# Pinning a program's first loads to program order and moving modulation rows and a broadcast behind them

## The chip, the cores and the metric

The kernel runs on one core of one Trainium2 chip. The metric is the device time of one execution in microseconds (us). Before the change it is 2306.07 us, the median of 3 runs (2305.83 to 2308.95).

## What is computed

A backbone of four layers over 256 latent tokens and 256 context tokens of width 1024, in float32. Each layer has a token mixer (chunked gated MLP, neighbourhood attention, mLSTM, chunked gated MLP) and a squared-ReLU MLP. Both are wrapped in RMSNorm and adaLN: a vector (c for the latent tokens, c_ctx for the context) passes a silu and a 1024 x 6144 matrix `ada_w`, and gives shift, scale and gate per layer:

```python
mod = [m[:, None, :] for m in jnp.split(c_act @ ada_w[i] + ada_b[i], 6, axis=-1)]
h = rmsnorm(x, norm_g[i, 0]) * (1.0 + mod[1]) + mod[0]
y = chunk_gmlp(h, ...)                       # layer 0
x = x + mod[2] * rmsnorm(y, norm_g[i, 1])
h = rmsnorm(x, norm_g[i, 2]) * (1.0 + mod[4]) + mod[3]
x = x + mod[5] * rmsnorm(sqrelu_mlp(h, ffn_w1[i], ffn_w2[i]), norm_g[i, 3])
```

So the first projection of layer 0 needs mod[0] and mod[1] of that layer for both vectors; mod[2] to mod[5] are needed later.

## The kernel before

The 512 tokens are four tiles of 128: two of context (`CTXT`), two latent (`LAT`). Weights arrive as tiles of 128 x 1024 float32 (512 KB): `raw`, four buffers. ScalarE copies such a tile to `whi` (rounded to float32r, L1288), VectorE computes the rest `wlo` (L1289), four buffers each; TensorE multiplies hi by hi, hi by lo and lo by hi (L391 to L393, one "step" of four token tiles is 24 matmuls of row blocks for two slices of 128). The activations are split in the same way into `hhi` and `hlo` (`split_h`, L336 and L337).

The modulation of a layer comes in two ways. By TensorE (`pe_items`, L200): `ada_w` itself is loaded into the same `raw` buffers and multiplied with silu(c) as a stationary operand of 32 columns; mod[0] and mod[1] of layer 0 come this way, in two groups `("s", 0)` and `("s", 1)` of eight raws, each group giving both mods for half of the channels. After a group, `ada_sum` (L222) copies the sum out of PSUM on ScalarE, `ada_fin` (L236 to L248) transposes it on TensorE and finishes on VectorE. By VectorE (`row_items`, L170): a transposed tile of `ada_w` (`row`, three buffers) is multiplied with `crow`, which is silu(c) broadcast to all partitions, and summed along the row; two such operations, one for each vector, make a block of 128 channels. mod[2], mod[3], mod[4] of layer 0 come this way, 24 tiles, spread over the first half of layer 0's mixer. `load_crow` (L146) loads c and c_ctx to 128 partitions, 512 KB each, and takes the silu.

The plan (`plan`) is a list of steps in program order. In layer 0: the first group's raws, sums of squares and transposes of the context tiles (`rows(CTXT)`, L1125 to L1143), loads and the same for the latent tiles, `apply` (modulate and split) for one half of the channels, the first two steps of the projection `gv` for the context tiles and then for the latent ones, with the second group's raws between, `apply` for the other half, and then the rest. The projection's results go through four PSUM buffers (`py`) that VectorE evacuates (L515). `emit` walks through the list and issues loads some steps ahead (`AHEAD`): list 0 holds the weights and the raws, list 1 the modulation rows.

Program order is not the order on an engine: a scheduler of the framework sorts the instructions of each queue by what it thinks is ready, loads and modulation rows too. Each queue then runs strictly in its order. Loads of the `raw` and `row` tiles go through SP's queue, some small ones and the two broadcasts of c through ScalarE's, bias rows through GpSimd's. A load on SP's or ScalarE's queue also takes one of eight semaphores in turn, and waits until the load that had it before has landed.

Of the kernel before, what the change touches and what calls it, by code (L numbers as in the profile page):

```python
# [8 lines left out]
F = mybir.dt.float32  # L9
# [14 lines left out]
CTXT = (0, 1)  # L24
LAT = (2, 3)
NB_HI = 4
NB_RAW = 4
NB_ROW = 3
LOOK = 3

AHEAD = (3, 2)
# [14 lines left out]

ON_PE = [(1, 5), (2, 5), (3, 2), (3, 5)]
FILLS = {(0, 0): (2, 2), (0, 1): (1, 1), (1, 0): (2, 1), (1, 1): (3, 2), (2, 0): (5, 0), (2, 1): (4, 0), (3, 0): (7, 0)}
XS1, XS2 = 2, 3
WAIT = 3  # L50
S2B, NUMB = 6, 2

# [10 lines left out]
class Net:  # L63
# [27 lines left out]

    def py(self):
        return self.pp.tile([128, 512], F, tag="py", bufs=4, name=self.name("py"))

    def w4(self):
        return self.sp.tile([128, 1024], F, tag="w4", bufs=2, name=self.name("w4"))
# [49 lines left out]
    def load_crow(self):  # L146

        for s in range(2):
            self.nc.scalar.dma_start(self.crow[:, s], self.bc(self.t["crow"][s]))
        self.nc.scalar.activation(self.crow, self.crow, AF.Silu)  # L150

    def new_mods(self, l):
# [950 lines left out]
    def plan(self):  # L1103
        nc, t = self.nc, self.t
        L = self.layers
        steps = []

        def load_xs(g):
            for i in g:
                if g == CTXT:  # L1110
                    x = self.w4()
                    self.xs[i] = [x[:, :512], x[:, 512:]]
                else:
                    self.xs[i] = [self.w2(), self.w2()]
                for h in range(2):
                    nc.sync.dma_start(self.xs[i][h], t["xin"][i][:, h * 512:(h + 1) * 512])

        def start():
            self.xs = {}
            load_xs(CTXT)  # L1120
            nc.sync.dma_start(self.ident, t["ident"])
            self.new_h()
            self.xT = self.ybuf()[:, :4096].rearrange("p (k n) -> p k n", k=8)

# [30 lines left out]

        first = self.pe_items(L[0], ("s", 0), True) + self.pe_items(L[0], ("s", 1), True)
        f0, f1 = first[:6], first[6:]
        steps += f0[:XS1] + [Step(lambda: load_xs(LAT))] + f0[XS1:XS2] + [Step(lambda: rows(CTXT))] + f0[XS2:]
        later = [x for u in ON_PE if u[0] in L for x in self.pe_items(*u)]

        def take(c):
# [5 lines left out]
        for n, l in enumerate(L):  # L1167
# [10 lines left out]
            for ph, w in phases:  # L1178
                ha, hb, body, ta, tb, close = ph
# [6 lines left out]
                if (l, w) in BESIDE:  # L1186
                    units, cnt, lo, hi = BESIDE[l, w]
                    body = spread(body, take(cnt) + [x for u in units for x in self.row_items(*u)], lo, hi)
                if n == 0 and w == 0:
                    body = [Step(self.load_crow)] + body  # L1190
                steps += before + ha + between + after + hb + body
                last = n == len(L) - 1 and w == 1
                pre = None if last else ((l, 1) if w == 0 else (L[n + 1], 0))
# [37 lines left out]
    def emit(self, steps):  # L1231
        nc, t = self.nc, self.t
# [7 lines left out]
        ops, nxt, cur = [], 0, -1  # L1240
        first = min(i for i, s in enumerate(steps) if s.key is not None) - WAIT
        slow = [steps.index(s) for s in self.slow]
# [7 lines left out]
        loads, at = ([], []), {}  # L1250
        for n, (o, a) in enumerate(ops):
            for r in [("w", a)] if o == "prep" else [("a", r) for r in steps[a].ada or []]:
                loads[r[0] == "a" and r[1][0] == "row"].append(r)
            at[n] = [len(x) - 1 for x in loads]
        raw, split, nl = {}, {}, [0, 0]
        for f in self.head:
            f()

        def load(r):
            if r[0] == "a" and r[1][0] == "row":  # L1260
                x = self.wp.tile([128, 1024], F, tag="row", bufs=NB_ROW, name=self.name("row"))
            else:
                x = self.wp.tile([128, 1024], F, tag="raw", bufs=NB_RAW, name=self.name("raw"))
            if r[0] == "w":
                nc.sync.dma_start(x, t["w"][r[1]])
            elif r[1][0] == "row":
                _, l, m, c = r[1]
                nc.sync.dma_start(x, t["adat"][l, m * 8 + c])
            else:
                l, m, k = r[1]  # L1270
                src = t["ada_w"][l, k * 128:(k + 1) * 128]
                if isinstance(m, tuple):
                    nc.sync.dma_start(x.rearrange("p (m n) -> p m n", m=2),
                                      src[:, :2048].rearrange("p (m n) -> p m n", m=2)[:, :, m[1] * 512:m[1] * 512 + 512])
                else:
                    nc.sync.dma_start(x, src[:, m * 1024:(m + 1) * 1024])
            raw[r] = x

        for n, (o, a) in enumerate(ops):
            for i in range(2):  # L1280
                while nl[i] < len(loads[i]) and nl[i] <= at[n][i] + AHEAD[i]:
                    load(loads[i][nl[i]])
                    nl[i] += 1
            if o == "prep":
                src = raw.pop(("w", a))
                hi = self.wp.tile([128, 1024], R, tag="whi", bufs=NB_HI, name=self.name("whi"))
                lo = self.wp.tile([128, 1024], R, tag="wlo", bufs=NB_HI, name=self.name("wlo"))
                nc.scalar.activation(hi, src, AF.Copy)  # L1288
                nc.vector.tensor_tensor(lo, src, hi.bitcast(F), op=OP.subtract)  # L1289
                split[a] = (hi, lo)  # L1290
            else:
                s = steps[a]
                if s.key is not None:
                    s.fn(*split[order[s.key]])
                elif s.ada:
                    s.fn(*[raw.pop(("a", r)) for r in s.ada])
                else:
                    s.fn()
# [146 lines left out]
```

## Time and profile before

| what | value |
|---|---|
| median of 3 runs | 2306.07 us |
| the profiled execution | 2313.39 us, of which 2311.4 us span from the first to the last instruction |
| TensorE busy | 2231.5 us (97%) |
| VectorE busy | 1548.9 us (67%) |
| ScalarE busy | 1039.9 us (45%) |
| GpSimd busy | 144.3 us (6%) |
| DMA | 371.94 MB, mean 161 GB/s |

Busy time of TensorE counts matmuls that wait for nothing but the one before. Its clock has two levels, granted by a throttle; the profile gives the granted clock of a stretch as a share of the full 2.4 GHz, and 0.50 is 1.2 GHz. The profiled execution is one of several and some us longer than the median; its stages are read for where time goes, not for the total.

### The profile page before, as it was taken

To read this page: it belongs to the slowest core of one execution; us is meant where nothing else is said; L and a number is where in the kernel's file an instruction comes from. 1 tells how busy PE (TensorE), PEld (TensorE's weight loads), DVE (VectorE), ACT (ScalarE), POOL (GpSimd) and SP (SyncE) were. 2 spreads that over 40 slices of the span, in tenths; PEclk is the share of its full clock that TensorE was granted. 3 is DMA by queue.
4 is the path that set the end of the run, shared out by engine and by line. 5 is a ranking of instruction groups with operands and counts; after the bars stand their busy time and mean duration, and the time that the engine had idled before them with its cause. 6 is when DMAs were issued, how large, how long until landed. Compare 5 with 4: busy or idle time off the path is not lost. (4 is left out here: it accounts for less than half of the span.)

```text
span 2311.4 us, 30189 instructions
## 1 busy us (share of the span) xinstructions
PE 2231.5 (97%) x11424; PEld 1830.1 (79%) x11424; DVE 1548.9 (67%) x2492; ACT 1039.9 (45%) x1770; POOL 144.3 (6%) x155
## 2 busy tenths in 40 slices
PE   6999999989999999999999999999999989998998
PEld 2888888878888877767888888777678968996987
DVE  4965354589973465776899433574688679677555
ACT  3544322353322354565633222535655556545543
POOL 0000000010000020111100000201100000001000
PEclk9999999999999999999999999998999999998999
DMA  8863333357763333222477433333378668565664
GB/s 290 270 195 98 92 90 95 128 160 255 242 200 100 92 125 117 67 60 66 163 249 240 130 98 98 120 119 103 107 256 288 187 194 314 176 182 162 189 188 131
DMA packets 111506, 371.94 MB, mean 161 GB/s; under 512 B 14161, under 2 KB 18529, under 8 KB 111361
## 3 DMA queue, kind: packets, MB, share of 16 engines
q1 hardware_dynamic: 104544, 351.97, 48.5%
q0 software_dynamic: 2960, 8.57, 1.4%
q10 hardware_dynamic: 3856, 9.47, 1.2%
q8 instruction: 89, 1.46, 0.3%
q14 instruction: 57, 0.46, 0.1%
HBM read 368.84 MB, written 1.13 MB: 160 GB/s over the span
## 5 line engine op out<-in xcount | busy, mean ns | idle before, releaser
L1289 DVE TENSOR_TENSOR wlo<-raw,whi 128x1024 fp32r<-128x1024 f32 x465 | 572.0, 1231 | 482.2 <-ACT whi L1288 476.1
L1288 ACT ACTIVATE whi<-raw 128x1024 fp32r<-128x1024 f32 x465 | 492.2, 1059 | 894.5 <-PE py L393 494.6
L376 PE MATMUL pa<-hhi,whi 128*128 128x256 f32 (+1 forms) x1704 | 570.3, 336 | 3.1 <-DVE w L903 2.5
L377 PE MATMUL pa<-hlo,whi 128*128 128x256 f32 (+1 forms) x1704 | 566.9, 333 | 1.1 <-DVE hlo L337 1.1
L378 PE MATMUL pa<-hhi,wlo 128*128 128x256 f32 (+1 forms) x1704 | 565.7, 332 | 0.0
L392 PE MATMUL py<-wlo,zh 128*128 128x512 f32 x1056 | 415.0, 393 | 0.0
L391 PE MATMUL py<-whi,zh 128*128 128x512 f32 x1056 | 413.4, 391 | 1.3 <-DVE y L423 0.8
L393 PE MATMUL py<-whi,zl 128*128 128x512 f32 x1056 | 411.8, 390 | 0.0
L170 DVE CUSTOM_DVE_ANT_0 w<-row,crow,rb 128x1024 f32<-128x1024 f32 x288 | 361.2, 1289 | 2.7 <-DMA row<-in_adat_dram 2.7
L376 PEld LDWEIGHTS pa<-hhi,whi 128*128 128x128 f32 x1704 | 322.7, 190 | 42.8 <-issue 6.5
L377 PEld LDWEIGHTS pa<-hlo,whi 128*128 128x128 f32 x1704 | 323.9, 190 | 32.4 <-DVE hlo L337 3.5
L378 PEld LDWEIGHTS pa<-hhi,wlo 128*128 128x128 f32 x1704 | 323.6, 190 | 30.3
L391 PEld LDWEIGHTS py<-whi,zh 128*128 128x128 f32 x1056 | 198.3, 188 | 47.4 <-ACT zh L578 1.6
L393 PEld LDWEIGHTS py<-whi,zl 128*128 128x128 f32 x1056 | 198.3, 188 | 42.8
L392 PEld LDWEIGHTS py<-wlo,zh 128*128 128x128 f32 x1056 | 198.4, 188 | 41.4
L391 PE MATMUL py<-whi,hhi 128*128 128x512 f32 x512 | 203.0, 399 | 5.3 <-ACT hhi L336 5.3
L393 PE MATMUL py<-whi,hlo 128*128 128x512 f32 x512 | 202.3, 397 | 1.7 <-DVE hlo L337 1.7
L392 PE MATMUL py<-wlo,hhi 128*128 128x512 f32 x512 | 202.3, 395 | 0.2 <-DVE wlo L1289 0.2
L391 PEld LDWEIGHTS py<-whi,hhi 128*128 128x128 f32 x512 | 97.4, 190 | 34.2 <-ACT hhi L336 7.6
L423 DVE TENSOR_TENSOR y<-py,y 128x512 f32<-128x512 f32 x132 | 87.3, 688 | 47.6 <-PE py L393 47.6
L393 PEld LDWEIGHTS py<-whi,hlo 128*128 128x128 f32 x512 | 97.4, 190 | 25.6 <-DVE hlo L337 3.8
L392 PEld LDWEIGHTS py<-wlo,hhi 128*128 128x128 f32 x512 | 97.4, 190 | 21.2 <-DVE wlo L1289 1.0
(234 smaller groups left out, 1936.7 us busy)
## 6 DMA issues: line engine op xcount, KB each, us to landing
raw<-in_w_dram SPq DMA_DIRECT2D x465, 512.0 KB, 4.2
row<-in_adat_dram SPq DMA_DIRECT2D x144, 512.0 KB, 4.5
raw<-in_ada_w_dram SPq DMA_DIRECT2D x48, 512.0 KB, 4.4
G<-gates ACTq DMA_DIRECT2D x12, 512.0 KB, 6.5
brow<-in_gmbv_dram POOLq DMA_DIRECT2D x12, 256.0 KB, 4.9
nab<-in_nabias_dram POOLq DMA_DIRECT2D x8, 384.0 KB, 3.4
w<-in_xin_dram SPq DMA_DIRECT2D x8, 256.0 KB, 6.6
x<-in_xin_dram ACTq DMA_DIRECT2D x4, 512.0 KB, 6.0
```

The costliest lines, as they stand in the source:

```text
L170: self.nc.vector.tensor_tensor_reduce(self.w4(), w, self.crow[:, s], 1.0, st["b"][:, c:c + 1], OP.mult, OP.add, self.mods[l][:, m, c, s:s ...
L376: nc.tensor.matmul(ps, whi[:, k], self.hhi[:, k, c0:c1], start=k == 0, stop=False)
L377: nc.tensor.matmul(ps, whi[:, k], self.hlo[:, k, c0:c1], start=False, stop=False)
L378: nc.tensor.matmul(ps, wlo[:, k], self.hhi[:, k, c0:c1], start=False, stop=k == 7)
L391: nc.tensor.matmul(ps, zh[:, c], whi[:, k], start=first and k == 0, stop=False)
L392: nc.tensor.matmul(ps, zh[:, c], wlo[:, k], start=False, stop=False)
L393: nc.tensor.matmul(ps, zl[:, c], whi[:, k], start=False, stop=last and k == 1)
L423: nc.vector.tensor_tensor(y, ps, y, op=OP.add)
L1288: nc.scalar.activation(hi, src, AF.Copy)
L1289: nc.vector.tensor_tensor(lo, src, hi.bitcast(F), op=OP.subtract)
```

## The change

Four edits. The first loads (x, the identity, and every load of list 0 that the plan issues up to the step `slow[1]`, the last `apply` of the context tiles) get `keep_in_program_order`, so that the scheduler leaves their order alone. `rows(CTXT)` moves to the very front of the plan and the loads of the latent tiles from after the second of the first group's steps to after the third. Modulation rows are only loaded once the walk is behind the step at which the mixer's body begins, and into each of the three `row` buffers VectorE first writes one element that it reads from `hhi[:, 7, 511]`, the last element of the last split of the head, so the load can't start earlier. The two broadcasts of c move from ScalarE's queue to GpSimd's and are held back in the same way. No computation is added beside the five one-element copies.

```diff
--- before.py
+++ after.py
@@ -46,7 +46,6 @@
 
 ON_PE = [(1, 5), (2, 5), (3, 2), (3, 5)]
 FILLS = {(0, 0): (2, 2), (0, 1): (1, 1), (1, 0): (2, 1), (1, 1): (3, 2), (2, 0): (5, 0), (2, 1): (4, 0), (3, 0): (7, 0)}
-XS1, XS2 = 2, 3
 WAIT = 3
 S2B, NUMB = 6, 2
 
@@ -92,6 +91,9 @@
     def py(self):
         return self.pp.tile([128, 512], F, tag="py", bufs=4, name=self.name("py"))
 
+    def inorder(self, ins):
+        return self.tc.keep_in_program_order(ins)
+
     def w4(self):
         return self.sp.tile([128, 1024], F, tag="w4", bufs=2, name=self.name("w4"))
 
@@ -146,7 +148,9 @@
     def load_crow(self):
 
         for s in range(2):
-            self.nc.scalar.dma_start(self.crow[:, s], self.bc(self.t["crow"][s]))
+
+            self.nc.vector.tensor_copy(self.crow[:, s, :1], self.hhi[:, 7, 511:512].bitcast(F))
+            self.nc.gpsimd.dma_start(self.crow[:, s], self.bc(self.t["crow"][s]))
         self.nc.scalar.activation(self.crow, self.crow, AF.Silu)
 
     def new_mods(self, l):
@@ -1113,12 +1117,12 @@
                 else:
                     self.xs[i] = [self.w2(), self.w2()]
                 for h in range(2):
-                    nc.sync.dma_start(self.xs[i][h], t["xin"][i][:, h * 512:(h + 1) * 512])
+                    self.inorder(nc.sync.dma_start(self.xs[i][h], t["xin"][i][:, h * 512:(h + 1) * 512]))
 
         def start():
             self.xs = {}
             load_xs(CTXT)
-            nc.sync.dma_start(self.ident, t["ident"])
+            self.inorder(nc.sync.dma_start(self.ident, t["ident"]))
             self.new_h()
             self.xT = self.ybuf()[:, :4096].rearrange("p (k n) -> p k n", k=8)
 
@@ -1155,7 +1159,7 @@
 
         first = self.pe_items(L[0], ("s", 0), True) + self.pe_items(L[0], ("s", 1), True)
         f0, f1 = first[:6], first[6:]
-        steps += f0[:XS1] + [Step(lambda: load_xs(LAT))] + f0[XS1:XS2] + [Step(lambda: rows(CTXT))] + f0[XS2:]
+        steps += [Step(lambda: rows(CTXT))] + f0[:3] + [Step(lambda: load_xs(LAT))] + f0[3:]
         later = [x for u in ON_PE if u[0] in L for x in self.pe_items(*u)]
 
         def take(c):
@@ -1187,7 +1191,8 @@
                     units, cnt, lo, hi = BESIDE[l, w]
                     body = spread(body, take(cnt) + [x for u in units for x in self.row_items(*u)], lo, hi)
                 if n == 0 and w == 0:
-                    body = [Step(self.load_crow)] + body
+                    self.body = Step(self.load_crow)
+                    body = [self.body] + body
                 steps += before + ha + between + after + hb + body
                 last = n == len(L) - 1 and w == 1
                 pre = None if last else ((l, 1) if w == 0 else (L[n + 1], 0))
@@ -1253,16 +1258,25 @@
                 loads[r[0] == "a" and r[1][0] == "row"].append(r)
             at[n] = [len(x) - 1 for x in loads]
         raw, split, nl = {}, {}, [0, 0]
+        at_slow = ops.index(("step", slow[1]))
+        at_body = ops.index(("step", steps.index(self.body)))
         for f in self.head:
             f()
 
-        def load(r):
+        nrow = [0]
+
+        def load(r, early):
+            io = self.inorder if early else lambda i: i
             if r[0] == "a" and r[1][0] == "row":
                 x = self.wp.tile([128, 1024], F, tag="row", bufs=NB_ROW, name=self.name("row"))
+                if nrow[0] < NB_ROW:
+
+                    nc.vector.tensor_copy(x[:, :1], self.hhi[:, 7, 511:512].bitcast(F))
+                nrow[0] += 1
             else:
                 x = self.wp.tile([128, 1024], F, tag="raw", bufs=NB_RAW, name=self.name("raw"))
             if r[0] == "w":
-                nc.sync.dma_start(x, t["w"][r[1]])
+                io(nc.sync.dma_start(x, t["w"][r[1]]))
             elif r[1][0] == "row":
                 _, l, m, c = r[1]
                 nc.sync.dma_start(x, t["adat"][l, m * 8 + c])
@@ -1270,16 +1284,16 @@
                 l, m, k = r[1]
                 src = t["ada_w"][l, k * 128:(k + 1) * 128]
                 if isinstance(m, tuple):
-                    nc.sync.dma_start(x.rearrange("p (m n) -> p m n", m=2),
-                                      src[:, :2048].rearrange("p (m n) -> p m n", m=2)[:, :, m[1] * 512:m[1] * 512 + 512])
+                    io(nc.sync.dma_start(x.rearrange("p (m n) -> p m n", m=2),
+                                         src[:, :2048].rearrange("p (m n) -> p m n", m=2)[:, :, m[1] * 512:m[1] * 512 + 512]))
                 else:
                     nc.sync.dma_start(x, src[:, m * 1024:(m + 1) * 1024])
             raw[r] = x
 
         for n, (o, a) in enumerate(ops):
             for i in range(2):
-                while nl[i] < len(loads[i]) and nl[i] <= at[n][i] + AHEAD[i]:
-                    load(loads[i][nl[i]])
+                while (i == 0 or n > at_body) and nl[i] < len(loads[i]) and nl[i] <= at[n][i] + AHEAD[i]:
+                    load(loads[i][nl[i]], n <= at_slow)
                     nl[i] += 1
             if o == "prep":
                 src = raw.pop(("w", a))
```

On SP's queue, in the first group, before (`raw` are the tiles of `ada_w`, `row` a modulation row's, `w` half tiles of the latent x):

```order
L1273 DMA raw_100<-in_ada_w_dram 128x2x512
L1273 DMA raw_102<-in_ada_w_dram 128x2x512
L1273 DMA raw_104<-in_ada_w_dram 128x2x512
L1268 DMA row_106<-in_adat_dram 128x1024
L1268 DMA row_108<-in_adat_dram 128x1024
L1273 DMA raw_115<-in_ada_w_dram 128x2x512
L1273 DMA raw_117<-in_ada_w_dram 128x2x512
L1116 DMA w_16_123<-in_xin_dram 128x512
L1116 DMA w_17_124<-in_xin_dram 128x512
L1116 DMA w_18_127<-in_xin_dram 128x512
L1116 DMA w_19_128<-in_xin_dram 128x512
L1273 DMA raw_131<-in_ada_w_dram 128x2x512
```

and now, from the same place on:

```order
L1287 DMA raw_100<-in_ada_w_dram 128x2x512
L1287 DMA raw_144<-in_ada_w_dram 128x2x512
L1287 DMA raw_146<-in_ada_w_dram 128x2x512
L1287 DMA raw_153<-in_ada_w_dram 128x2x512
L1287 DMA raw_155<-in_ada_w_dram 128x2x512
L1287 DMA raw_161<-in_ada_w_dram 128x2x512
L1279 DMA raw_163<-in_w_dram 128x1024
L1120 DMA w_26_169<-in_xin_dram 128x512
L1120 DMA w_27_170<-in_xin_dram 128x512
L1120 DMA w_28_173<-in_xin_dram 128x512
L1120 DMA w_29_174<-in_xin_dram 128x512
L1279 DMA raw_177<-in_w_dram 128x1024
```

The rows and the latent tiles stood ahead of the first group's last raw (raw_131); now the group's raws (to raw_161) follow each other, then come the first projection weight, the latent tiles and the second weight.

On TensorE, from the last raw of the first group on, before (`pada` is the sum of a group, `pa` with `ident` a transpose, `py` the projection):

```order
L200 MATMUL pada_110<-raw_131,cs 32x512 x2
L236 MATMUL pa_211<-ident,mp_206 128x128 x4
L1137 MATMUL pa_269<-ident,w_16_123 128x128 x4
L1137 MATMUL pa_276<-ident,w_17_124 128x128 x4
L1137 MATMUL pa_283<-ident,w_18_127 128x128 x4
L1137 MATMUL pa_290<-ident,w_19_128 128x128 x4
L200 MATMUL pada_312<-raw_183,cs 32x512
L391 MATMUL py_240<-whi_191,hhi_93 128x512
L392 MATMUL py_240<-wlo_192,hhi_93 128x512
```

and now, some rows later in the same stretch, from the second weight's first matmul on:

```order
L395 MATMUL py_236<-whi_193,hhi_93 128x512
L395 MATMUL py_243<-whi_193,hhi_93 128x512
L204 MATMUL pada_308<-raw_179,cs 32x512
L396 MATMUL py_236<-wlo_194,hhi_93 128x512
L397 MATMUL py_236<-whi_193,hlo_94 128x512
L1141 MATMUL pa_265<-ident,w_26_169 128x128 x4
L1141 MATMUL pa_272<-ident,w_27_170 128x128 x4
L1141 MATMUL pa_279<-ident,w_28_173 128x128 x4
L395 MATMUL py_236<-whi_193,hhi_93 128x512
L396 MATMUL py_236<-wlo_194,hhi_93 128x512
L1141 MATMUL pa_286<-ident,w_29_174 128x128 x4
L397 MATMUL py_236<-whi_193,hlo_94 128x512
```

The four groups of latent transposes stood between the first group's end (the transpose of mp_206) and the first projection matmul; now they stand between the matmuls of the second projection weight.

On TensorE, around the end of the second group, before:

```order
L200 MATMUL pada_312<-raw_333,cs 32x512 x2
L391 MATMUL py_341<-whi_197,hhi_93 128x512
L392 MATMUL py_341<-wlo_198,hhi_93 128x512
L393 MATMUL py_341<-whi_197,hlo_94 128x512
L391 MATMUL py_348<-whi_197,hhi_93 128x512
L236 MATMUL pa_373<-ident,w_79_371 128x128 x4
L392 MATMUL py_348<-wlo_198,hhi_93 128x512
L393 MATMUL py_348<-whi_197,hlo_94 128x512
L391 MATMUL py_348<-whi_197,hhi_93 128x512
L392 MATMUL py_348<-wlo_198,hhi_93 128x512
L393 MATMUL py_348<-whi_197,hlo_94 128x512
L391 MATMUL py_240<-whi_365,hhi_93 128x512
```

and now:

```order
L397 MATMUL py_344<-whi_193,hlo_94 128x512
L204 MATMUL pada_308<-raw_315,cs 32x512 x2
L395 MATMUL py_344<-whi_193,hhi_93 128x512
L396 MATMUL py_344<-wlo_194,hhi_93 128x512
L397 MATMUL py_344<-whi_193,hlo_94 128x512
L204 MATMUL pada_308<-raw_329,cs 32x512 x2
L240 MATMUL pa_369<-ident,w_77_367 128x128 x4
L395 MATMUL py_236<-whi_361,hhi_93 128x512
L396 MATMUL py_236<-wlo_362,hhi_93 128x512
L395 MATMUL py_243<-whi_361,hhi_93 128x512
```

Behind the second group's last raw (raw_333) stood nine more matmuls of the latent tiles; now its counterpart, raw_329, is followed by the transpose of its own sum and by the projection that needs it.

On ScalarE the silu of the broadcasts (L150) moves from the twelfth row to behind the evacuated latent tiles of the projection's first group, with a table load ahead of it and one behind. On VectorE six row operations leave the head; from some 200 instructions on, the order on each engine is the same as before.

## Rows read from the trace of the kernel before

**Rows 1.** page of the profile, busy us (share of span) and instructions

```profile
PE 2231.5 (97%) x11424; PEld 1830.1 (79%) x11424; DVE 1548.9 (67%) x2492; ACT 1039.9 (45%) x1770; POOL 144.3 (6%) x155
```

**Rows 2.** windows: length, busy us by engine, then clock, DMA share, GB/s

```profile
22.20:28.70 6.50, 2.10 (x8) 0.29 (x8) 5.20 (x12) 2.89 (x8) 0.54 (x1) 0.92 1.05 396
57.80:400.00 342.20, 342.20 (x1576) 284.56 (x1577) 201.92 (x287) 135.04 (x213) 8.10 (x13) 1.00 0.45 141
```

**Rows 3.** TensorE's timeline (start, us, waited for); second row: groups, 13.3 to 22.2

```profile
13.40 3.18 PE L200 MATMUL pada<-raw,cs 128*32 128x512 f32 x8 [13.40 <-DMA raw<-in_ada_w_dram]
L1137 PE MATMUL pa<-ident,w 128*128 128x128 f32 x16 | 2.7, 302 | 0.0
28.70 1.92 PE L200 MATMUL pada<-raw,cs 128*32 128x512 f32 x4 [2.99 <-DMA raw<-in_ada_w_dram]
36.78 0.50 PE L391 MATMUL py<-whi,hhi 128*128 128x512 f32 x1 [0.55 <-ACT hhi L336]
52.74 1.05 PE L200 MATMUL pada<-raw,cs 128*32 128x512 f32 x4
57.76 0.50 PE L391 MATMUL py<-whi,hhi 128*128 128x512 f32 x1 [1.24 <-ACT hhi L336]
```

**Rows 4.** DMA landings up to 60 us: the raws (L1273), the broadcasts of c

```profile
DMA to landing us min/median/max: 3.7/6.7/9.6
crow<-in_crow_dram ACTq DMA_DIRECT2D x2, 512.0 KB, 7.8
```

**Rows 5.** timeline of ScalarE and VectorE, the latent tiles' sums and scaling

```profile
26.13 0.63 ACT L297 ACTIVATE junk<-w 128x512 f32<-128x512 f32 x1
26.88 0.63 ACT L297 ACTIVATE junk<-w 128x512 f32<-128x512 f32 x1
29.41 0.88 DVE L1134 TENSOR_SCALAR w<-w,col 128x512 f32<-128x512 f32 x2 [0.66 <-POOL col L303]
```

**Rows 6.** windows as in rows 2: TensorE's gaps, and the clock behind some

```profile
56.50:57.70 1.20, 0.02 (x1) 0.00 (x0) 1.20 (x3) 1.20 (x4) 0.00 (x0) 1.00 0.55 218
1540.00:1542.00 2.00, 0.00 (x0) 0.00 (x0) 1.91 (x5) 0.79 (x2) 0.50 (x1) 1.00 0.02 4
1543.50:1546.50 3.00, 3.00 (x16) 3.00 (x16) 2.97 (x9) 0.72 (x3) 1.46 (x2) 0.50 0.22 77
1594.50:1608.00 13.50, 13.50 (x47) 9.47 (x44) 4.54 (x21) 6.21 (x22) 0.00 (x0) 0.50 0.15 43
```

**Rows 7.** VectorE: one window (length, busy), then its timeline

```profile
70.00:140.00 70.00, 69.85 (x108) 1.00 0.81 261
...
64.42 1.28 DVE L337 TENSOR_TENSOR hlo<-y,hhi 128x512 fp32r<-128x512 f32 x2
76.01 1.23 DVE L1289 TENSOR_TENSOR wlo<-raw,whi 128x1024 fp32r<-128x1024 f32 x1
77.14 1.28 DVE L170 CUSTOM_DVE_ANT_0 w<-row,crow,rb 128x1024 f32<-128x1024 f32 x1
78.35 1.28 DVE L170 CUSTOM_DVE_ANT_0 w<-row,crow,rb 128x1024 f32<-128x1024 f32 x1
...
87.94 1.29 DVE L515 TENSOR_TENSOR v<-py,brow 128x512 f32<-128x512 f32 x2
```

**Rows 8.** timeline of ScalarE and GpSimd; DMA from 57 to 145 us

```profile
63.12 1.28 ACT L517 ACT_TABLE_LOAD   x1
71.83 0.62 ACT L517 ACTIVATE v<-v 128x512 f32<-128x512 f32 x1
85.57 1.06 ACT L1288 ACTIVATE whi<-raw 128x1024 fp32r<-128x1024 f32 x1 [4.38 <-PE py L393]
92.00 0.54 POOL L103 DMA_DIRECT2D brow<-in_gmbv_dram  x1 [6.76 <-DVE v L515]
DMA packets 7128, 23.31 MB, mean 265 GB/s; under 512 B 1006, under 2 KB 1518, under 8 KB 7122
brow<-in_gmbv_dram POOLq DMA_DIRECT2D x4, 256.0 KB, 4.2
```

## The prediction, made before the changed kernel ran

> **What bounds the kernel now.** I read the table of engines first: TensorE is busy 2231.5 us of a 2311.4 us span [rows 1], so a change pays only where TensorE stands idle or runs slowly. The windows by stage say where that is near this change [rows 2]: 2.10 us of work in the 6.5 us from 22.2 to 28.7, after nothing at all before the first matmul at 13.40 [rows 3]; and then one unbroken stretch, 342.20 of 342.20 us from 57.8 to 400. In that stretch nothing but TensorE sets the time. So the question is one number, the moment at which the first matmul of the unbroken stretch starts: 57.76 us. Call it Q. If Q moves, the end moves as far, as long as the stretch behind it stays unbroken and at the same clock.
>
> The timeline of TensorE shows what Q is made of [rows 3]. The adaLN matmuls take their weights in tiles of 512 KB, "raws", eight in a first group and eight in a second. The first pair waits for its load until 13.40; the last of the first group waits 2.99 us for its load and starts at 28.70. In that wait the DMA engines are full (share 1.05, 396 GB/s [rows 2]), so bytes count there. Then comes a chain through ScalarE and VectorE to the first projection matmul at 36.78, then a mix of projection and second-group matmuls, whose last raw starts at 52.74, then a second chain to Q.
>
> **The change part by part.**
>
> *Bytes in front of the first group.* Ahead of the last raw's load stand, besides what it needs, two broadcasts of c (512 KB each), two modulation rows (512 KB each) and four half tiles of the latent x (256 KB each): 3.15 MB. All of it goes behind. If bytes alone decided, the last raw would start 3.15 MB / 396 GB/s = 7.9 us earlier, at 20.8. There is a second limit, the four buffers of the raws. First raw: 13.40 less 1.05 MB of broadcasts at 396 GB/s (2.7 us) gives 10.7. Two raws take 3.18 us at the start, so 13.9. The sixteen transposes of the context tiles (2.7 us together) now stand before the end of the third raw (1.05): 17.6. Fourth raw: 18.65. The seventh raw's load waits for the third's buffer and lands no sooner than 3.7 us after its issue [rows 4], so it runs from 21.3 to 22.35; the eighth needs the fourth's buffer, 18.65 + 3.7, and starts at 22.4. I take 22.4, because by then the queue ahead is empty, which is nearest to the shortest landing; with the median of 6.7 it is 25.4. Term: **-6.3** (bounds -7.9 and -3.3).
>
> *Its own time.* At 28.70 the raw took 1.92 us where 1.05 is usual [rows 3], at a clock that had fallen in the wait (0.92 on average from 22.2 to 28.7). The new wait before it is short: **-0.9**.
>
> *From there to the first projection matmul.* Before: 28.70 + 1.92 = 30.62 to 36.78, 6.16 us, with the sixteen latent transposes in front. These move behind it, so I take the same chain as at the second group, 52.74 + 1.05 = 53.79 to 57.76, 3.97 us: **-2.2**. The first projection matmul would start at 27.4, 9.4 us earlier.
>
> *What comes back between there and Q.* The transposes return, now in TensorE's row behind the first projection matmuls: **+2.7**, as those of the context tiles. Half a raw that stood ahead stands behind: **+0.5**. The latent tiles' sums and scalings now run beside TensorE's first projection matmuls. After the first of these ScalarE still has one activation split (0.6), four sums 0.75 apart and a weight split (1.06), 4.7 us; then VectorE takes a small step, waits 0.66 for GpSimd, scales two half tiles in 0.88 and copies a transposed block between them (0.64), 2.4 us: 7.1 in all [rows 5, 7, 8]. TensorE has 18 projection matmuls (24 take 5.44 us [rows 8]: 4.1), half a raw (0.5) and twelve transposes (2.0) ahead of the last latent ones, 6.6: **+0.5** of waiting (bounds 0, if it is covered, and 3.0, the four sums uncovered).
>
> *The second chain loses its cover.* Before, nine latent projection matmuls stood behind the last raw of the second group and ran during its chain; TensorE idled only 1.24 us before Q. Now all of them stand ahead of that raw, so the chain is bare: 3.97 less 0.7 for four transposes is 3.3 of idling, **+2.1**.
>
> *The clock after a bare gap.* Where TensorE did almost nothing for 1.20 us, at 56.5, the granted clock stayed at 1.00. Where it did nothing from 1540 to 1542, the clock was 0.50 (1.2 GHz instead of 2.4) from 1543.5 to 1546.5; another spell, from 1594.5 to 1608, lasted 13.5 us [rows 6]. Q would now follow a gap of the second kind, and what follows Q is bound by TensorE alone. A spell of 3 us at half speed costs **+1.5** (bounds 0 and 6.8, for no spell and one of 13.5 us).
>
> *Modulation rows later.* Six row operations (1.28 us each) leave the head and run in the stretch from 58 on, where VectorE is already full (69.85 of 70 us) while TensorE never waits for it [rows 2, 7]. Cover: the four PSUM buffers of the projection. A group of four tiles lasts TensorE 21.8 us (four steps of 5.44: ScalarE's split at 85.57 follows 4.38 us of idling and a split of 1.06 [rows 8]); VectorE then has twelve row operations at 1.21 from start to start, four splits at 1.13 and four evacuations at 0.64 [rows 7], 21.6 us. It keeps pace but hardly catches up. So: **0**, if it starts in time.
>
> *The broadcast of c later.* VectorE's first row operation now waits for ScalarE's silu; behind it on VectorE stand weight splits and the evacuations of the second group of tiles, for which TensorE waits. The latest harmless start: the last step of that group begins at 85.57 and lasts 5.44, so TensorE asks for the first buffer again at 91.0, Q + 33.2; eight row operations, three splits and one evacuation (13.7 us) go before it: Q + 19.5. The expected start: the last split of the activations ends at 65.70, Q + 7.9 [rows 7]; two issues on GpSimd at 0.54 make it Q + 9.0; a landing of 4.2 us, as for the smaller broadcasts on that queue, gives Q + 13.2, one of 7.8, as for these same broadcasts in the head, Q + 16.8 [rows 4, 8]. ScalarE is through with the evacuated tiles at 72.45 (Q + 14.7), loads a table (1.28) and takes about 1.9 for the silu (twice the columns of a weight split of 1.06): Q + 17.9 to Q + 18.7. That is 0.8 to 1.6 us of room: **0** (bounds 0 and +5.3, below). Behind the silu on ScalarE wait weight splits that TensorE needs a group later, and the second table load; its idle time there covers them (4.38 us before a split). The five one-element copies on VectorE have no like in the trace; a whole evacuation takes 0.64, so all five stay under 3.2 us, and they stand where VectorE would wait for the broadcast anyway.
>
> A rule speaks against this step. On GpSimd's queue the broadcasts of the bias rows landed in a median of 4.2 us while VectorE had 0.15 us free in 70 [rows 7, 8]: no delay is seen. The Trainium skill, SBUF — State Buffer, section "SBUF: two separate sides", says that a DMA issued from GpSimd can be held back while VectorE runs copies in its fast mode, since GpSimd then can't write the descriptors. By the row the step costs nothing; by the rule the sum would be that of the third rival.
>
> **Sum:** -6.3 - 0.9 - 2.2 + 2.7 + 0.5 + 0.5 + 2.1 + 1.5 = **-2.1 us**. Against the profiled execution's own 2313.39 us that is 2311.3; the median of the runs shown lies 7.3 us lower, at 2306.07, so the forecast is **2304.0**. A measurement of this kernel can tell about 0.2%, 4.6 us, from no change.
>
> **The rivals.**
>
> *The clock holds and the loads come early; faster.* Without the slow spell (-1.5), with the last raw at the bound by bytes (another -1.6) and the latent chain covered (-0.5): -5.7, 2300.4. For it: the DMA engines do reach 396 GB/s in the head, and the gap of 1.20 us left the clock alone. Against it: the four buffers, and the spell after the gap at 1540.
>
> *All of the early start is kept,* -9.4, 2296.7: the latent rows and the second group would have to hide fully. Against it: TensorE's row is in a fixed order, and the work is the same.
>
> *The broadcast lands late; slower.* With both broadcasts, three rows and two weight tiles under way (3.67 MB) at the stretch's mean of 265 GB/s [rows 8], the last lands 13.8 us after its issue, at Q + 22.8; with the silu VectorE starts at Q + 24.8, and TensorE waits 5.3 us for a PSUM buffer. It decides from a landing of about 8.5 us on; the price is 1 us for each, paid once. -2.1 + 5.3 = +3.2: 2309.3. For it: the room is only 0.8 to 1.6 us. Against it: the small broadcasts of that stretch land in 4.2 us. What the page named above says of GpSimd's queue would work the same way.
>
> *A long spell at half clock behind Q; slower.* As from 1594.5 to 1608: +6.8 in place of +1.5, so +3.2: 2309.3. The trace has spells of both lengths, the short one right behind a bare gap.
>
> *The change does not move Q.* If a landing and not the bytes sets the first raw and the order alone changes: 2306.
>
> **How the numbers follow.** Forecast 0.57; early loads and full clock 0.22; all kept 0.03; late broadcast 0.10; long spell 0.05; no effect 0.03. Faster by over 0.2% (under 2301.5): most of the second case, all of the third, a little of the first, 0.24. Slower by over 0.2% (over 2310.7): the upper parts of the two slow cases, 0.07. Within: 0.69. The range from 2300.0 to 2309.0 leaves out the third case, a part of the second and the upper half of the slow ones, together under 0.2.
>
> **What would show it.** Right: the first adaLN matmul near 10.7, the eighth raw near 22.4, the first projection matmul near 27.4, the second group's last raw near 50, Q near 54, after some 3.3 us of idling and followed by some 3 us at clock 0.50; no wait of TensorE from there to 400. Wrong: raws that still wait for full DMA engines near 20, a projection that waits for the latent transposes for over 3 us, a clock that stays at 1.00, or a wait of TensorE for VectorE 33 us behind Q.

## The result: slower, and the profile after

The changed kernel took 2321.94 us (median of 4 runs) beside 2305.95 us of the kernel before: ratio 1.0054, 95% interval 1.0034 to 1.0073. Run again beside other kernels, 12 runs against 35 of before gave 2314.61 us against 2309.12, ratio **1.0029 (1.0015 to 1.0043)**. The change makes the kernel slower, by 3.5 to 9.9 us by the larger sample; 2304.0 was forecast, with faster or the same at 0.93. Two runs that lie far outside all others (4448.66 us of the last kernel in the table below, 12510.37 us of before beside it) are left out of that kernel's ratio.

The page's table of engines after the change, as [rows 1]: TensorE's work is 5.5 us longer (spells, stretches at granted clock 0.50, count as busy), the span 9.6 us.

```profile
span 2321.0 us, 30201 instructions
...
PE 2237.0 (96%) x11424; PEld 1834.2 (79%) x11424; DVE 1547.6 (67%) x2497; ACT 1042.2 (45%) x1772; POOL 144.7 (6%) x157
```

TensorE's timeline after (start, length, instruction, count, [idle before it <- what ended that]); these rows answer to [rows 3], the last but one to 57.76:

```profile
11.12 3.19 PE L204 MATMUL pada<-raw,cs 128*32 128x512 f32 x8 [11.12 <-DMA raw<-in_ada_w_dram]
14.25 2.79 PE L1141 MATMUL pa<-ident,w 128*128 128x128 f32 x12
...
23.48 3.43 PE L204 MATMUL pada<-raw,cs 128*32 128x512 f32 x8 [3.03 <-DMA raw<-in_ada_w_dram]
...
30.67 0.80 PE L395 MATMUL py<-whi,hhi 128*128 128x512 f32 x1 [2.40 <-ACT hhi L340]
...
52.45 1.05 PE L204 MATMUL pada<-raw,cs 128*32 128x512 f32 x4
...
57.27 0.50 PE L395 MATMUL py<-whi,hhi 128*128 128x512 f32 x1 [2.40 <-ACT hhi L340]
...
94.85 0.47 PE L395 MATMUL py<-whi,hhi 128*128 128x512 f32 x1 [2.94 <-DVE v L519]
```

Three things are to be seen. The loads did come earlier (first matmul 11.12, before 13.40; last raws of the first group 23.48, before 28.70). Nearly nothing of it reached Q, the start of the unbroken stretch: 57.27, before 57.76. And the stretch is no longer unbroken: at 94.85, Q + 37.6, TensorE has waited 2.94 us for VectorE. The windows (length, busy us by engine, granted clock, DMA share, GB/s) show the clock behind each gap, and VectorE full while TensorE waits:

```profile
24.00:26.50 2.50, 2.50 (x8) 0.19 (x4) 0.00 (x0) 0.00 (x0) 0.00 (x0) 0.50 0.99 354
31.00:33.50 2.50, 2.50 (x7) 1.97 (x7) 1.31 (x4) 2.47 (x7) 0.54 (x1) 0.50 1.00 330
58.00:61.00 3.00, 3.00 (x9) 2.30 (x8) 3.00 (x5) 3.00 (x5) 0.00 (x0) 0.50 0.62 175
...
92.00:94.50 2.50, 0.00 (x0) 0.00 (x0) 2.50 (x4) 0.00 (x0) 0.00 (x0) 1.00 0.75 241
95.50:98.50 3.00, 3.00 (x9) 2.35 (x8) 3.00 (x5) 3.00 (x9) 0.50 (x1) 0.50 0.66 240
```

Each spell lasts some 3.4 us and costs half of that, 1.7 us: two in the head (they are inside Q; both profiles of before have 6.8 us at 0.50 there too, from about 28 to 35 us), one behind Q, one behind the wait at 92 us. Why VectorE was late is in its timeline, and in ScalarE's and GpSimd's:

```profile
66.48 0.21 DVE L152 COPY crow<-hhi 128x1 f32<-128x1 f32 x2
...
66.93 1.14 POOL L153 DMA_DIRECT2D crow<-in_crow_dram  x2 [30.90 <-DVE acc L523]
...
77.71 1.28 ACT L154 ACT_TABLE_LOAD   x1 [4.55 <-DMA crow<-in_crow_dram]
...
79.00 1.92 ACT L154 ACTIVATE crow<-crow 128x2048 f32<-128x2048 f32 x1
...
80.95 1.28 DVE L174 CUSTOM_DVE_ANT_0 w<-row,crow,rb 128x1024 f32<-128x1024 f32 x1 [7.62 <-ACT crow L154]
```

The landing of the two halves, for the line that issues them:

```profile
DMA to landing us min/median/max: 6.9/8.5/10.1
```

The gate (the copies from the last split of the head, for which the broadcast and the rows wait) opens at 66.48, Q + 9.2. The broadcast is issued on GpSimd at once and its second half lands 10.1 us after its issue. Only then does ScalarE begin the table load; table and silu take 3.2 us, and VectorE begins its row operations at 80.95, Q + 23.7, after 7.62 us of idling. From there to 160 us it is busy 9.6 us or more in every 10, and the evacuations that TensorE needs queue behind the rows.

### The profile page after: what moved, and what is told of

Same layout as the page of the kernel before. It is cut to its first block, busy times and chain, and to the rows that moved or that the text cites. A ratio compares the mean times of both kernels' runs of the same rounds, so it can differ in the third digit from the quotient of the medians.

```text
span 2321.0 us, 30201 instructions
## 1 busy us (share of the span) xinstructions
PE 2237.0 (96%) x11424; PEld 1834.2 (79%) x11424; DVE 1547.6 (67%) x2497; ACT 1042.2 (45%) x1772; POOL 144.7 (6%) x157
## 5 line engine op out<-in xcount | busy, mean ns | idle before, releaser
L396 PEld LDWEIGHTS py<-wlo,hhi 128*128 128x128 f32 x512 | 99.5, 194 | 24.2 <-DVE wlo L1303 2.5
```

What stands on the lines that cost most here:

```text
L396: nc.tensor.matmul(ps, zh[:, c], wlo[:, k], start=False, stop=False)
```

## The experiments

Each was run in 12 runs beside the kernel before. One table for all, from the results and one profile of each. The wait is TensorE's for VectorE, between 60 and 170 us; the start of the row operations is counted from Q.

| kernel | ratio to before (95%) | Q | rows start at Q + | wait |
|---|---|---|---|---|
| before, two profiles | 0.9993 (0.998 to 1.0006) | 57.76, 56.00 | 7.9 (second) | 0 |
| changed, two profiles | 1.0029 (1.0015 to 1.0043) | 57.27, 55.31 | 23.7, 24.7 | 2.9, 4.0 |
| broadcast put back | 1.0005 (0.9993 to 1.0018) | 57.55 | 14.4 | 0 |
| pinning alone | 1.0021 (1.0007 to 1.0034) | 56.36 | 8.6 | 0 |
| waits alone | 1.0015 (1.0001 to 1.0028) | 56.36 | 23.8 | 2.8 |
| broadcast at half the apply | 0.9991 (0.9979 to 1.0002) | 55.38 | 14.4 | 0 |
| rows without the wait | 0.999 (0.9979 to 1.0002) | 57.47 | 19.8 | 0 |
| broadcast back, gaps filled | 0.9999 (0.9987 to 1.0012) | 57.73 | 13.9 | 0 |
| half the apply, gaps filled | 1.0004 (0.9992 to 1.0017) | 57.95 | 13.1 | 0 |
| the same, deeper first group | 0.9977 (0.9961 to 0.9992) | 51.96 | 13.1 | 0 |
| the same, both groups deeper | **0.9969 (0.9954 to 0.9984)** | 51.33 | 13.2 | 0 |
| changed, deeper first group | 1.0006 (0.9993 to 1.0019) | 53.86 | 24.1 | 3.1 |

### Both kernels once more

> The kernel before, unchanged, once more: a second profile of it and the scatter between runs. Every theory expects 2306 us (2301.9 to 2309.0 so far). What it settles is how far two profiles of one kernel differ behind 160 us, where both kernels issue the same instructions: between the two profiles at hand 3.8 us of the 9.6 us difference appear only there.

> The changed kernel, unchanged, once more, with as many runs as the others. Theory A (the late broadcast costs 2.9 us of waiting and 1.7 us at half clock near 92 us, the head as good as nothing, and the rest of what was measured is the scatter of the later half-clock spells): 4.6 us above the kernel with the broadcast put back (2308.7), 2313 to 2315. Theory C (something further behind 160 us is systematic): 2320 or more again, with most profiles and clocks showing the long spell near 1600 us.

The second profile of before has a span of 2302.2 us, the first 2311.4: 9.2 us between two profiles of one kernel. The clock explains most of it (mean 0.990 against 0.987, 7 us of 2306). The largest piece: where the first shows 13.5 us at 0.50 [rows 6], behind a wait of 1.92 us, the second waits 1.72 us at the same instruction and keeps its clock. The timeline of the first, then the timeline and a window of the second:

```profile
1593.91 1.57 PE L959 MATMUL pa<-y,kw 128*64 128x129 f32 x16 [1.92 <-DVE kw L952]
```

```profile
1592.10 1.10 PE L959 MATMUL pa<-y,kw 128*64 128x129 f32 x16 [1.72 <-DVE kw L952]
```

```profile
1590.00:1605.00 15.00, 13.28 (x77) 9.98 (x76) 9.81 (x33) 11.61 (x36) 1.09 (x2) 1.00 0.34 90
```

Of the fourteen profiles of this record three have a spell of 13.5 us or more near 1600 us: the first of before, the first of the changed kernel and the one of pinning alone. So Theory C falls, as far as these profiles reach: the long spell comes with either kernel, and the changed kernel's first profile was unlucky there. Its second profile (span 2312.2) gives the account with less noise:

```profile
22.58 1.05 PE L204 MATMUL pada<-raw,cs 128*32 128x512 f32 x4 [1.65 <-DMA raw<-in_ada_w_dram]
...
28.84 0.79 PE L395 MATMUL py<-whi,hhi 128*128 128x512 f32 x1 [2.40 <-ACT hhi L340]
...
55.31 0.50 PE L395 MATMUL py<-whi,hhi 128*128 128x512 f32 x1 [2.40 <-ACT hhi L340]
...
80.01 1.28 DVE L174 CUSTOM_DVE_ANT_0 w<-row,crow,rb 128x1024 f32<-128x1024 f32 x1 [8.64 <-ACT crow L154]
...
93.91 0.77 PE L395 MATMUL py<-whi,hhi 128*128 128x512 f32 x1 [3.97 <-DVE v L519]
```

Q 0.7 us earlier than in the second profile of before, a spell behind it (+1.7), the wait (+4.0), a spell behind that (+1.7): +6.7 us, and 0.29% of 2306 is 6.7. That the two agree so closely is luck: the interval of the measured loss is 3.5 to 9.9 us, and two profiles of one kernel have their Q 1.8 to 2.0 us apart.

### The change in parts

```
broadcast put back:  load_crow as before (ScalarE's queue, no copy ahead); rows and pinning as changed
pinning alone:       the same, and no copies ahead of the rows, no `n > at_body`
waits alone:         the changed kernel without keep_in_program_order, with the step order of XS1, XS2
```

> The changed kernel with the broadcast of silu(c) put back as before: on ScalarE's queue, with no wait; rows still wait for the head, loads still pinned. Theory A (the late broadcast starves VectorE, then TensorE): VectorE's row operations start with the rows' landing, near 72 us in place of 80.95, TensorE has no wait for VectorE near 92 us and no half-clock spell behind it, 2.9 + 1.7 = 4.6 us less: 2317. Theory B (what the change costs comes from the pinned loads and the gaps at the head): the time stays at 2322. Both: the 1 MB of the broadcast then lies among the first adaLN blocks and can cost up to 2.6 us at 390 GB/s.

> Only the pinned loads and the moved steps of the changed kernel; the rows and the broadcast are loaded as before, with no waits. Theory A: no wait of TensorE for VectorE near 92 us, about 2317 or less. Theory B: as slow as the changed kernel, 2322, with a half-clock spell behind the first projection matmul and one behind the long stretch's first matmul (1.7 us each).

> Only the waits: the rows and the broadcast wait for the head as in the changed kernel, while the first loads and the steps stand as in the kernel before. Theory A: the wait of TensorE for VectorE comes some 34 us behind the long stretch's first matmul, 4.6 us more than before: 2310.5; less if the head gains what the rows and the broadcast (4 x 0.5 MB, 1.3 us each) no longer take from the first adaLN blocks. Theory B: as before, 2306, or faster by those landings.

Theory A holds. With the broadcast put back the rows start at 71.91, without a wait of VectorE, TensorE waits for nothing from 60 to 170 us, and the loss is gone (2308.7, not 2317: the 2322 it was reckoned from was itself too high). The waits alone bring the wait back; TensorE's waits in that stretch (total, times, longest) are one line:

```profile
PE py L396 <- DVE v L520: 2.8, 1, 2.8
```

Theory B was put as all or nothing, and pinning alone does not fit either: no wait near 92 us, a spell behind Q, and still 1.0021. Its Q of 56.36 and that spell explain 0.3 or 2.1 us, by which profile of before one takes; 4.8 were measured (1.6 to 7.8). Its profile also has the long spell near 1592 us, which comes and goes between profiles of one kernel. The clocks of its runs narrow the rest: their mean is 0.9868, that of the 35 runs of before beside them 0.9885, and 0.0017 of 2309 us is 4.0 us (give or take 2.6). So about all of this loss is a lower clock and not waiting. Why its runs had more time at half clock than those of the kernel with the broadcast put back (0.9885, with the same two spells ahead of and behind Q) stays open.

### The broadcast: when, and beside what

```
broadcast at half the apply:  copy from hhi[:, 3, 255:256] right behind the first apply; silu where it was
rows without the wait:        no copies ahead of the rows, no `n > at_body`; the broadcast waits as changed
```

> The changed kernel, but the broadcast of silu(c) waits only for the first half of the first apply (near 31 us) instead of the last element of the head (62 us); it stays on GpSimd's queue. Theory A (the time of the broadcast decides): it lands near 38 us, VectorE's rows start with the rows' own landing near 72 us, no wait of TensorE near 92 us: 2308, as with the broadcast put back. Theory D (GpSimd's queue is what is slow, wherever it stands): landing 8 to 10 us after its issue here too, but early enough all the same, so the landing and not the time tells A from D.

> The changed kernel, but the first modulation rows load as early as before (no wait for the head); the broadcast alone waits. Theory A with the bytes setting the landing: the broadcast has 1.5 MB less beside it, lands some 4 us sooner (73 in place of 77 us), VectorE's rows start near 76.5 us, 19 us behind the long stretch's first matmul, just inside the 19.5 us that the prediction worked out as the room: TensorE's wait near 92 us shrinks from 2.9 to under 0.5 us, the spell behind it goes, and the time comes to about 2309. Theory D: it lands near 77 us as before, the wait stays at 2.9, and the time stays with the changed kernel's.

Both take the wait away. The second says why the broadcast was slow. DMA transfers (instruction, count, KB each, median us to landing) behind the gate, first in the changed kernel from 66 to 78 us, then with the rows loaded long before, from 67 to 76 us:

```profile
row<-in_adat_dram SPq DMA_DIRECT2D x3, 512.0 KB, 6.8
crow<-in_crow_dram POOLq DMA_DIRECT2D x2, 512.0 KB, 8.5
raw<-in_w_dram SPq DMA_DIRECT2D x2, 512.0 KB, 8.3
```

```profile
crow<-in_crow_dram POOLq DMA_DIRECT2D x2, 512.0 KB, 4.4
raw<-in_w_dram SPq DMA_DIRECT2D x2, 512.0 KB, 4.5
```

These are medians; the second half of the broadcast took 10.1 us (11.2 in the changed kernel's second profile) and 4.7. With the three rows out of the way, the same broadcast on the same queue lands in 4.4 us instead of 8.5, and the weights beside it in 4.5 instead of 8.3. It is the bytes that are let go together, not GpSimd's queue: Theory D falls.

The kernel with the rows loaded long before also sits just inside the edge. Its rows start at 77.23, Q + 19.8, and TensorE does not wait. Where it does wait, start less wait is Q + 20.7 to 21.0 in four profiles (23.7 - 2.9, 24.7 - 4.0, 23.8 - 2.8, 24.1 - 3.1). By these the room is some 20.8 us, and behind it each us costs one.

### The gaps and the clock

```
+ pj = self.pa()                         # in ada_fin, behind the group's own four transposes
+ for c in range(14): nc.tensor.transpose(pj[...], mp[...], self.ident[:n, :n])
```

> The kernel with the broadcast put back, and 14 more 128x128 transposes behind each of the two groups' own four, into a PSUM tile that nobody reads: they fill the 2.4 us in which TensorE waits for ScalarE's hhi ahead of the first projection matmul and of the long stretch's first matmul. If the idle time of these waits is what lets the clock fall: no half-clock spell behind either, 1.7 us each, the long stretch starts 1.7 us earlier, 2305 in all. If the spells come from the load (the first wide matmuls) and not from the wait: both spells stay, 2308.7.

> The kernel whose broadcast waits for the first half of the first apply only, with the 14 idle transposes behind each group's own four. If the two remaining spells at the head (behind 28.6 us and behind the long stretch's first matmul) are worth their 1.7 us each: the long stretch starts about 1.7 us earlier than 55.4 us and runs at clock 1.00 from its start, 3.4 us less than without the transposes: 2305 where the kernel before gives 2309. If the half speed that the first spell takes is only turned into waits for the second group's loads: 1.7 us less, 2307.

In the windows of the first of them the same 3 us behind the first projection matmul and behind Q now run at full clock, with 13 matmuls in place of 8 and 9:

```profile
29.30:31.00 1.70, 1.69 (x16) 1.45 (x14) 1.40 (x7) 1.20 (x3) 0.00 (x0) 1.00 1.03 410
32.00:35.00 3.00, 3.00 (x13) 2.33 (x14) 1.80 (x5) 2.97 (x7) 0.54 (x1) 1.00 0.97 327
...
58.00:61.00 3.00, 3.00 (x13) 2.11 (x13) 3.00 (x6) 3.00 (x5) 0.00 (x0) 1.00 0.57 180
```

So at these two places it is the idle time that lets the clock fall. The 3.4 us of gain did not show in the time of either kernel: part of the first went into waits for the second group's raws (0.3 and 0.5 us at 45.78 and 48.22), and the head's own scatter is as large (the second kernel's first projection matmul stands at 31.03, its twin's without the transposes at 28.60). The runs' clocks say the same: with the gaps filled the first kernel's mean is 0.9895 and that of before beside it 0.9883, worth 2.7 us (give or take 2.6), and its time is still that of before, so what the clock gave back came back as waiting. That these two spells go is shown, that it pays is not.

### The raw buffers

```
- x = self.wp.tile(..., tag="raw", bufs=NB_RAW, ...)
+ row = nl[0] in (4, 5, 6)               # both groups: also 14, 15, 16, and + 3 for 9 < nl[0] < 18
+ x = self.wp.tile(..., tag="row" if row else "raw", bufs=NB_ROW if row else NB_RAW, ...)
  ... nl[i] <= at[n][i] + AHEAD[i] + (3 if i == 0 and nl[0] < 8 else 0)
```

> The same, and the fifth, sixth and seventh adaLN block of the first group load into the three row buffers that are empty until the head has ended, so that they need not wait for a raw buffer. If the raw buffers are what holds the first group (the step of the prediction that put the eighth block at 22.4 us): the eighth block lands by 18 us, the group's last matmul ends near 21.5 in place of 24.8 us, the first projection matmul starts near 25.3 in place of 28.6 us. The long stretch then starts 3.3 us earlier too, 2302, unless the second group's blocks, whose buffers still come free one by one, become the bound: then it moves by 1 us or less, 2304.

> The same for both groups: the second group's fifth to seventh block go into row buffers too. If the second group's buffers are the bound behind the first group's: the long stretch starts 2 to 3 us before that of the kernel where only the first group has the extra buffers. If TensorE's own order (blocks between projection matmuls) is the bound: no difference between the two.

> The changed kernel with one edit: the fifth to seventh block of the first group load into the three empty row buffers. If the two costs add (the raw buffers at the head, the late broadcast behind it): the long stretch starts near 52 us, 3.3 us earlier than the 55.3 us of the changed kernel's second profile, VectorE's rows still start some 24 us behind it, TensorE still waits 3 to 4 us for VectorE there with a half-clock spell behind it, and the time is 2311, 0.1% above the kernel before instead of 0.29%. If an earlier head only lengthens the wait for the broadcast: 2314.

SyncE's queue issues the eight raws over 9.85 us instead of 15.86 (the changed kernel, second profile), and the whole head follows; the timeline of the kernel with the deeper first group:

```profile
3.88 15.86 SPq L1287 DMA_DIRECT2D raw<-in_ada_w_dram  x8
```

```profile
4.09 9.85 SPq L1294 DMA_DIRECT2D raw<-in_ada_w_dram  x8
...
21.00 1.05 PE L206 MATMUL pada<-raw,cs 128*32 128x512 f32 x4 [0.31 <-DMA raw<-in_ada_w_dram]
...
25.81 0.50 PE L401 MATMUL py<-whi,hhi 128*128 128x512 f32 x1 [0.88 <-ACT hhi L346]
...
51.96 0.50 PE L401 MATMUL py<-whi,hhi 128*128 128x512 f32 x1 [0.88 <-ACT hhi L346]
```

Against its twin without the edit Q moves from 57.95 to 51.96, 6.0 us, and the ratio from 1.0004 to 0.9977, 6.2 us (give or take 4.6): what Q gains here reaches the end, as far as the runs can tell. The 6.0 is more than the 3.3 expected because the twin's profile is a slow one: its last two raws waited 2.81 us and then ran at half clock, 1.7 us. Against the kernel with the broadcast at half the apply (Q 55.38) Q gains 3.4. The second group's extra buffers give 0.6 us of Q (1.3 counted from the first projection matmul), less than the 2 to 3 expected, and no difference in the time that the runs can tell. The last kernel shows that the two costs add: the changed kernel with the deeper first group has its first projection matmul at 25.64 and still waits 3.1 us for VectorE (Q came to 53.86 and not to 52: this profile's head ran at half clock for 6.8 us, from 24.2 on); 1.0006 instead of 1.0029. The kernel with the early broadcast, the filled gaps and both groups deeper is faster than before: 2300.85 us beside 2309.67, 0.31% (0.16 to 0.46).

## Why the prediction was wrong, step by step

- **First raw, 10.7.** Measured 11.12 and 11.60. Right within a us.
- **Eighth raw at 22.4, group done at 23.45.** Measured 26.9 (23.48 + 3.43) and 25.08 (24.03 + 1.05). The reason was right (four buffers), the size was off. The third raw was forecast to end at 17.6 and ended about 19.1 and 18.3: its second half stands behind the last four transposes, and in the first profile the twelve ahead of it took 2.79 us (1.57 in the second). So the seventh was issued at 19.61 and 18.85; it landed 3.9 and 3.7 us later, as forecast, but the eighth 4.7 (second profile). In the first profile the last two raws then ran at half speed. 1.6 to 3.5 us of the 9.4 were lost here. The kernels with row buffers show the limit: lifting it moved the eighth raw to 21.0. That buffers and not bytes held the raws is seen in the first profile too, where no byte moves just ahead of the seventh's issue (length, TensorE's busy us, clock, DMA share, GB/s):

```profile
19.00:20.00 1.00, 1.00 (x14) 1.00 0.00 0
```

- **Chain of 3.97 to the first projection matmul.** Measured 3.76 in both. Right.
- **First projection matmul to Q.** The terms gave 26.8; measured 26.6 and 26.5. But 1.7 of that is a half-clock spell behind the first projection matmul that the prediction did not have (it looked for one behind Q alone), so the terms for what comes back were 1.7 us too large together. The 0.5 us of waiting for the latent tiles' sums is one of them: TensorE waited for nothing there.
- **Q near 54.** 57.27 and 55.31; before itself has 57.76 and 56.00. First with first and second with second, the gain is 0.5 and 0.7 us, not 3.6; crosswise it is 2.4 and -1.3, so Q's gain is known to some 2 us. That one profile's Q carries an uncertainty of 2 us I had not allowed for.
- **Half-clock spell behind Q, +1.5.** Measured 1.7. Right.
- **Broadcast later, 0.** This step made the loss. (Without it the measured terms still add up to +1.0: the forecast gain had already gone in the steps above.) What failed first is the landing: 4.2 us, the row of the small broadcasts in the old stream [rows 8], and at most 7.8 [rows 4], for a transfer that the same change releases together with three rows, 2.6 MB behind one gate. Measured 10.1 and 11.2 us; 4.7 once the rows are not there. Second, the prediction let ScalarE load the table while the broadcast was still under way; the load began only behind the landing (77.71, after 4.55 us of waiting), 1.28 us more. Third, the second half was issued at Q + 10.2 and not Q + 9.0. The room was 1.3 us larger than reckoned (20.8). The bound of this step was there, and the rival's numbers were nearly those measured: start at Q + 24.8 (23.7 and 24.7 measured), wait 5.3 us (2.9 and 4.0, with a spell of 1.7 behind it: 4.6 and 5.7). That is luck in part, since its landing of 13.8 us was too long, and it too left the table load out. It got a chance of 0.10 where it should have been the forecast, with a spell added behind the wait.
- **The rule on GpSimd's descriptors** (the Trainium skill, SBUF — State Buffer, section "SBUF: two separate sides": a DMA issued from GpSimd can be held back while VectorE copies in its fast mode) was weighed beside that rival. The trace does not bear it out here: VectorE stood idle from 73.3 us on, 4 us before the late broadcast landed, while the DMA engines were full (share 1.03, 415 GB/s to 77.7), and the same transfer on the same queue took half as long once the rows were gone, with VectorE busy for 2.9 of the 5.3 us to its landing.

The sum with the measured sizes of the second profiles: -0.7 + 1.7 + 4.0 + 1.7 = +6.7 us in the place of -2.1. Of the 8.8 us between them 5.7 are the broadcast's, 2.9 Q's and 0.2 the spell's behind Q.

## What to carry to other kernels

When a change lets several loads wait for one event, sum the bytes that the event lets go and price the landing of the last of them; a landing taken from the quiet stream is the best case. An in-order engine's latest harmless start is worth working out from its backlog (19.5 us here, 20.8 measured), and a step that leaves a room of one us behind a wait that nobody has measured should not be priced at nothing. Loads that are first in the queue are not early while they wait for a buffer: look who frees it, and whether other buffers stand empty meanwhile.

## What the runs showed of the hardware

The granted clock can fall behind short gaps. After 2.40 to 2.83 us of waiting, with 0.66 us of transposes and about 0.70 us of waiting ahead of it, it was 0.50 for 3.4 or 6.8 us in each profile that had this bare gap ahead of the first projection matmul or of Q; 1.24 us of waiting [rows 3] left it alone in both profiles of before, and transposes that nobody reads held it at 1.00. But the length of the wait does not settle it. Near 1540 us all fourteen profiles have a wait of 2.34 to 2.39 us, and eleven of them a spell of 3.4 us behind it; the first of the changed kernel and those of the two kernels with nothing but the gaps filled beside the broadcast have none. Near 1594 us the wait is 1.65 to 1.93 us: behind 1.92 and 1.93 the clock was at 0.50 for 13.5 us or more, behind 1.88 not at all, and the first profile of the changed kernel has such a spell 1.7 us behind a wait of 1.69. So two profiles of one kernel can differ by 9 us, and the place of a loss has to be read from the head, not from the spans.
